# High and low weight products in pairs, first loads in halves, and dummy products at the start of a two-layer encoder

## The chip, the core and the metric

The kernel runs on one core of a Trainium2 chip. The metric is the device time of one execution in microseconds (us): 1684.95 us is the median of three runs of the kernel before (1684.54 to 1685.41). The core has a matrix engine (TensorE, in the profile PE for its products and PEld for its weight loads), VectorE (DVE), ScalarE (ACT), GpSimd (POOL) and a queue that issues transfers (SP). Products are summed in PSUM, everything else lies in SBUF, weights and inputs come from HBM by DMA.

## What is computed

Two layers of an encoder over 256 positions of 2048 channels, each a normalisation, one wide input projection, two groups of mixers and one output projection with a residual. Cut to the parts that set the work:

```python
def even_layer(h, w_in, w_out, ...):                      # w_in: 2048 x 14336
    a_q, a_i, a_ff, a_fb, a_g, b_u, b_g = split_cols(h @ w_in, EV_SIZES)
    a_out = hgrn2_mixer(a_q, a_i, a_ff, a_fb, lb, hgrn_nw) * jax.nn.silu(a_g)
    b_out = fourier_mixer(b_u, fw, fb) * jax.nn.silu(b_g)
    return jnp.concatenate([a_out, b_out], axis=-1) @ w_out   # 4096 x 2048

def odd_layer(h, w_in, w_out, ...):                       # w_in: 2048 x 13376
    c_in, c_b, c_c, c_g, d_z, d_xbc, d_dt = split_cols(h @ w_in, OD_SIZES)
    c_out = c_b * centred_dwconv(c_c * c_in, sconv_w) * jax.nn.silu(c_g)
    d_out = ssd_mixer(d_xbc, d_dt, d_z, ...)
    return jnp.concatenate([c_out, d_out], axis=-1) @ w_out

for layer in range(2):
    x = x + (even_layer if layer % 2 == 0 else odd_layer)(rms_norm(x, norm_w[layer]), ...)
return rms_norm(x, final_norm_w)
```

All of it is float32.

## The kernel before

**Two parts of each number.** The large products are made with a rounded 32-bit type. So that they stay exact enough, every weight and every activation is split in two: a high part (the rounded number) and a low part (what is left). A product then has three pieces: high weight by high activation, high weight by low activation, low weight by high activation. The activations of the first layer stand in the tile `xx`, 16 k tiles of 128 channels, each with its high half (256 positions) and its low half side by side. The mixers' outputs stand in `mm` in the same form.

**Weights come in halves.** `halves` lists all weight pieces in the order of their use: 562 pieces of 128 x 1024 numbers (512 KB), each being eight k tiles of 128 x 128. `load()` (L113) issues the transfer of a piece into one of five `raw` buffers from SP. `fetch()` (L121) makes the two parts of it: ACT copies `raw` into `hi` (L132), DVE subtracts to get `lo` (L133). There are three `hi`/`lo` buffer pairs (`NHL`), so ACT can write the high part of piece n + 3 only when the products have read that of piece n for the last time. `half()` (L152) hands out the next piece, runs whatever was put off with `later(n, ...)` to this piece, and fetches up to four pieces ahead.

**Three shapes of large product.** In `gemm_half` (L161) the weights are the stationary operand: for one piece, eight products of a high tile with 512 columns of `xx` (the high and the low activations together, L164), then eight products of a low tile with the 256 high activations (L167). All sixteen add into one PSUM bank. `gemm` calls it twice, `proj` gives a fresh bank. The even layer has 96 such projections (`pq`, two `pz`, `pu`, `pg`, `pbg`), the odd layer 105; so there are 402 calls of `gemm_half` and 3216 pairs of one high and one low product. The other two shapes have the activations stationary and always stream 512 columns of weights: the values `pv` (L508) and the output projections in `tproduct` (L183).

**Order.** Each engine runs its own list of instructions in order; a scheduler builds the lists from the program, so the written order is not always the order on an engine. Eight turns of `hp` make the even layer; each has, every other turn, `pv`, then for two heads `pq`, `pz`, `pz`, then `pu` twice, `pg` twice and `pbg` twice. Small products of the mixers (128 x 128, in plain float32) stand between the projections: `sa`/`sb`, `po`, `pt`, `fp`, `fm`, `fy`.

**The start.** SP issues `parT` (the small parameters, L258), then the first weight pieces and the eight chunks `x0` to `x7` of the input in turn (L263, L265). ACT and DVE split weights (L132, L133) and multiply the chunks by the norm weights into the two halves of `xx` (`split_by`, L223 and L224). ACT later squares the chunks in place for the norm (L276). The first products are those of `pv`: a unit of twelve for each piece, eight units.

Of the kernel before, what the change touches and what calls it, by code (L numbers as in the profile page):

```python
# [8 lines left out]
F32 = mybir.dt.float32  # L9
F32R = mybir.dt.float32r  # L10
U32 = mybir.dt.uint32
AF = mybir.ActivationFunctionType
ALU = mybir.AluOpType
ADD, SUB, MUL, MIN, MAX = ALU.add, ALU.subtract, ALU.mult, ALU.min, ALU.max

P = 128
# [40 lines left out]
def encoder_kernel(ctx: ExitStack, tc, xT, xN, w_ev, w_evo, w_od, w_odo, fw, fnr, par, con, acon, tric, outN):  # L57
    nc = tc.nc
    V, S, PE = nc.vector, nc.scalar, nc.tensor

    cpool = ctx.enter_context(tc.tile_pool(name="cpool", bufs=1))
# [9 lines left out]
    parT = cpool.tile([P, NPAR], F32, tag="par", name="parT")  # L71
# [7 lines left out]
    def pcol(name, i):  # L79
        return parT[:, PCOL[name] + i:PCOL[name] + i + 1]  # L80
# [9 lines left out]
    def t2(name, shape=(2, L)):  # L90
        return lpool[0].tile([P, *shape], F32, tag="t2", name=name, bufs=N2)

    def psum(tag, name, bufs, shape=(512,)):
        return ps.tile([P, *shape], F32, tag=tag, name=name, bufs=bufs)
# [4 lines left out]
    def paux(name, shape=(512,)):  # L99
        return psum("px", name, 8 - NPM, shape)  # L100
# [4 lines left out]
    n = 2 * (112 + 32)  # L105
# [2 lines left out]
    state = {"load": 0, "next": 0, "use": 0}  # L108
    HK = KT // 2
    NRAW, NHL, AHEAD = 5, 3, 4  # L110
    endp = []

    def load():  # L113
        n = state["load"]
        state["load"] = n + 1
        src, i, h = halves[n]
        raw = wpool.tile([P, HK * P], F32, tag=f"raw{n % NRAW}", name=f"raw{n}")
        nc.sync.dma_start(out=raw, in_=src[i][:, h * HK * P:(h + 1) * HK * P])
        loaded[n] = raw

    def fetch():  # L121
        n = state["next"]
        state["next"] = n + 1
        if n >= state["load"]:
            load()
        raw = loaded.pop(n)
        kept = n - (len(halves) - 8)
        i = n % NHL if kept < 0 else kept % (2 * NHL)
        pool = wpool if i < NHL else endp[0]
        hi = pool.tile([P, HK * P], F32R, tag=f"hi{i}", name=f"hi{n}")  # L130
        lo = pool.tile([P, HK * P], F32R, tag=f"lo{i}", name=f"lo{n}")
        S.activation(hi, raw, AF.Copy)  # L132
        V.tensor_tensor(lo, raw, hi.bitcast(F32), SUB)  # L133
        ready[n] = (hi, lo)

    def later(n, fn):
# [15 lines left out]
    def half():  # L152

        n = state["use"]
        due(n)
        while state["next"] <= min(n + AHEAD, len(halves) - 1):
            fetch()
        state["use"] = n + 1
        return ready.pop(n)

    def gemm_half(out, a, k0, first, last):  # L161
        hi, lo = half()
        for k in range(HK):
            PE.matmul(out, lhsT=hi[:, k * P:(k + 1) * P], rhs=a[:, k0 + k].rearrange("p s n -> p (s n)"),  # L164
                      start=(first and k == 0), stop=False)
        for k in range(HK):
            PE.matmul(out[:, :L], lhsT=lo[:, k * P:(k + 1) * P], rhs=a[:, k0 + k, 0], start=False,  # L167
                      stop=(last and k == HK - 1))

    def gemm(out, a):  # L170

        for h in range(2):
            gemm_half(out, a, h * HK, h == 0, h == 1)
# [43 lines left out]
    def split_by(dst, src, w=None):  # L217

        if w is None:
            S.activation(dst[:, 0], src, AF.Copy)  # L220
            V.tensor_tensor(dst[:, 1], src, dst[:, 0].bitcast(F32), SUB)
        else:
            S.activation(dst[:, 0], src, AF.Copy, scale=w)  # L223
            V.scalar_tensor_tensor(dst[:, 1], src, w, dst[:, 0].bitcast(F32), MUL, SUB)  # L224
# [30 lines left out]
    lay = ExitStack()  # L255
    ap_ = lay.enter_context(tc.tile_pool(name="ap", bufs=1))
    lpool.append(ap_)
    nc.sync.dma_start(out=parT, in_=par)  # L258
    V.memset(epsT, EPS)
    xcs = []  # L260
    for c in range(8):
        if c % 2 == 0:
            load()  # L263
        xc = t2(f"x{c}")
        nc.sync.dma_start(out=xc, in_=xT[:, 2 * c:2 * c + 2, :])  # L265
        xcs.append(xc)
    for c in range(8):
        if c % 2 == 0:
            fetch()
        for k in range(2):  # L270
            split_by(xx[:, 2 * c + k], xcs[c][:, k, :], pcol("nw0", 2 * c + k))
# [24 lines left out]
    with lay:  # L296
# [203 lines left out]
        for hp in range(8):  # L500
            if hp % 2 == 0:
                pv = [pmain(f"pv{hp}_{b}") for b in range(2)]
                for u in range(8):
                    hi, lo = half()
                    for k in range(2):
                        for b in range(2):
                            for n, (s_, w) in enumerate(((0, hi), (0, lo), (1, hi))):
                                PE.matmul(pv[b], lhsT=xx[:, 2 * u + k, s_, b * P:(b + 1) * P],  # L508
                                          rhs=w[:, k * 4 * P:(k + 1) * 4 * P], start=(u == 0 and k == 0 and n == 0),
                                          stop=(u == 7 and k == 1 and n == 2))  # L510
# [5 lines left out]
            for i in range(2):  # L516
                h = 2 * hp + i
# [15 lines left out]
            for i in range(2):  # L533
                h = 2 * hp + i
# [6 lines left out]


    ss1 = sp.tile([P, 2, 4], F32, tag="ss1", name="ss1")
    ones = cpool.tile([P, P], F32, tag="ones", name="ones")
    nc.gpsimd.memset(ones, 1.0)
    op = ctx.enter_context(tc.tile_pool(name="op", bufs=1))

    def tok(name, bufs=4):
# [27 lines left out]
    with ExitStack() as lay:  # L576
# [54 lines left out]
        for h in range(2):  # L631
            for out in (dtp, first_b):
                gemm_half(out, xx, h * HK, h == 0, h == 1)
# [300 lines left out]
```

## Time and profile before

| | us |
|---|---|
| median of three runs | 1684.95 |
| the profiled execution, whole | 1684.59 |
| its span on the core | 1682.8 |
| TensorE busy (PE) | 1666.2 (99%) |
| weight loads (PEld) | 1443.0 (86%) |
| VectorE busy | 1247.6 (74%) |
| ScalarE busy | 950.2 (56%) |
| bytes moved | 319.65 MB, mean 190 GB/s |

The span runs from the first to the last instruction of the program; 1.8 us of the profiled execution lie outside it. Busy times are unions of the instructions' stretches. Products are pipelined: one starts before the one ahead has ended, so the distance from start to start is what a product costs, and a busy share of 99% does not by itself say that each product is as short as it can be.

### The profile page before, as it was taken

The page shows a single profiled execution, that of the slowest core. Times are in us where ns is not written, and L with a number is a line of the kernel's source. Part 1 is how long each engine was busy: PE and PEld are TensorE (multiplying, and loading weights), DVE is VectorE, ACT ScalarE, POOL GpSimd, SP SyncE. Part 2 cuts the span into 40 slices and gives each one's busy share as a digit, 9 for nine tenths or more (in the row PEclk, how much of TensorE's full clock was granted, in tenths as well). Part 3 has the DMA queues.
Part 4 walks back from the last instruction along what each step waited for, and adds up shares of the span by engine and source line. Part 5 has one row for each costly group of instructions (what it writes and reads, how often), then busy time and mean ns, then how long its engine had stood idle before and what let it go on. Part 6 is the DMA issues. An engine that isn't in the chain of part 4 may idle for free.

```text
span 1682.8 us, 24794 instructions
## 1 busy us (share of the span) xinstructions
PE 1666.2 (99%) x9216; PEld 1443.0 (86%) x9216; DVE 1247.6 (74%) x2187; ACT 950.2 (56%) x1593; POOL 1.8 (0%) x13
## 2 busy tenths in 40 slices
PE   8999999999999999999999999999999999999997
PEld 6888888888888888888888888888888888888886
DVE  7868677867786788754548998888898797865554
ACT  6656555655665565644445576666665565654443
POOL 0000000000000000000000000000000000000000
PEclk9999999999999999999999999999999999999999
DMA  8555555545445545476665667656656655576553
GB/s 304 173 179 174 167 171 179 171 167 186 166 158 180 191 154 178 158 223 206 213 212 191 205 218 200 195 191 203 197 185 201 196 193 179 178 238 209 195 192 123
DMA packets 97977, 319.65 MB, mean 190 GB/s; under 512 B 10880, under 2 KB 19520, under 8 KB 97728
## 3 DMA queue, kind: packets, MB, share of 16 engines
q1 hardware_dynamic: 97856, 318.07, 57.5%
q8 instruction: 72, 1.18, 0.3%
q14 instruction: 49, 0.40, 0.1%
HBM read 313.77 MB, written 4.26 MB: 189 GB/s over the span
## 4 chain that ended last, share of the span: by engine, by line
PE 99%; DMA 0%; ACT 0%; DVE 0%; ACTq 0%; issue 0%; SPq 0%
PE pz L164 10%; PE o L183 10%; PE pz L167 5%; PE pv L508 5%; PE oD L183 5%; PE oC L183 5%; PE px L164 4%; PE pbg L164 4%; PE pq L164 4%; PE pcb L164 4%; PE pu L164 4%; PE pci L164 4%; PE pcg L164 3%; PE pcc L164 3%; PE pg L164 3%; PE pci L167 2%
## 5 line engine op out<-in xcount | busy, mean ns | idle before, releaser
L133 DVE TENSOR_TENSOR lo<-raw,hi 128x1024 fp32r<-128x1024 f32 x562 | 686.0, 1223 | 383.1 <-ACT hi L132 379.4
L132 ACT ACTIVATE hi<-raw 128x1024 fp32r<-128x1024 f32 x562 | 594.8, 1059 | 552.7 <-PE o L183 88.4
L164 PE MATMUL pz<-xx,hi 128*128 128x512 f32 x768 | 192.4, 393 | 0.0
L164 PEld LDWEIGHTS pz<-xx,hi 128*128 128x128 f32 x768 | 138.2, 189 | 24.5
L183 PE MATMUL o<-hi,mm 128*128 128x512 f32 x512 | 126.9, 390 | 0.0
L183 PEld LDWEIGHTS o<-hi,mm 128*128 128x128 f32 x512 | 95.8, 188 | 19.7
L167 PEld LDWEIGHTS pz<-xx,lo 128*128 128x128 f32 x768 | 104.8, 191 | 7.5
L167 PE MATMUL pz<-xx,lo 128*128 128x256 f32 x768 | 107.1, 283 | 0.0
L508 PE MATMUL pv<-hi,xx 128*128 128x512 f32 x256 | 81.9, 399 | 7.0 <-ACT xx L223 7.0
L183 PE MATMUL o<-lo,mm 128*128 128x512 f32 x256 | 68.5, 389 | 0.0
L164 PE MATMUL pbg<-xx,hi 128*128 128x512 f32 x256 | 66.2, 400 | 0.0
L164 PE MATMUL pcb<-xx,hi 128*128 128x512 f32 x256 | 65.5, 398 | 0.0
L164 PE MATMUL pg<-xx,hi 128*128 128x512 f32 x256 | 65.4, 398 | 0.0
L164 PE MATMUL px<-xx,hi 128*128 128x512 f32 x256 | 65.3, 397 | 0.0
L164 PE MATMUL pu<-xx,hi 128*128 128x512 f32 x256 | 64.8, 395 | 0.0
L164 PE MATMUL pci<-xx,hi 128*128 128x512 f32 x256 | 64.8, 395 | 0.0
L183 PE MATMUL oC<-hi,mm 128*128 128x512 f32 x256 | 64.5, 389 | 0.0
L164 PE MATMUL pq<-xx,hi 128*128 128x512 f32 x256 | 64.5, 394 | 0.0
L164 PE MATMUL pcc<-xx,hi 128*128 128x512 f32 x256 | 64.1, 393 | 0.0
L164 PE MATMUL pcg<-xx,hi 128*128 128x512 f32 x256 | 64.1, 393 | 0.0
L508 PEld LDWEIGHTS pv<-hi,xx 128*128 128x128 f32 x256 | 49.2, 192 | 17.3 <-ACT xx L223 7.0
L183 PE MATMUL oD<-hi,mm 128*128 128x512 f32 x256 | 63.4, 390 | 0.0
(551 smaller groups left out, 2851.0 us busy)
## 6 DMA issues: line engine op xcount, KB each, us to landing
raw<-in_w_ev SPq DMA_DIRECT2D x224, 512.0 KB, 3.9
raw<-in_w_od SPq DMA_DIRECT2D x210, 512.0 KB, 4.4
raw<-in_w_evo SPq DMA_DIRECT2D x64, 512.0 KB, 4.5
raw<-in_w_odo SPq DMA_DIRECT2D x64, 512.0 KB, 4.5
ab<-rd SPq DMA_DIRECT2D x64, 128.0 KB, 4.9
x<-in_xT SPq DMA_DIRECT2D x8, 256.0 KB, 6.9
fw<-in_fw SPq DMA_DIRECT2D x8, 256.0 KB, 5.9
xr<-in_xN SPq DMA_DIRECT2D x8, 256.0 KB, 5.8
```

The costliest lines, as they stand in the source:

```text
L132: S.activation(hi, raw, AF.Copy)
L133: V.tensor_tensor(lo, raw, hi.bitcast(F32), SUB)
L164: PE.matmul(out, lhsT=hi[:, k * P:(k + 1) * P], rhs=a[:, k0 + k].rearrange("p s n -> p (s n)"), start=(first and k == 0), stop=False)
L167: PE.matmul(out[:, :L], lhsT=lo[:, k * P:(k + 1) * P], rhs=a[:, k0 + k, 0], start=False, stop=(last and k == HK - 1))
L183: PE.matmul(outs[b], lhsT=a[:, k0 + 2 * u + k, s_, b * P:(b + 1) * P], rhs=w2[part][:, k * 4 * P:(k + 1) * 4 * P], start=(u == 0 and part ...
L508: PE.matmul(pv[b], lhsT=xx[:, 2 * u + k, s_, b * P:(b + 1) * P], rhs=w[:, k * 4 * P:(k + 1) * 4 * P], start=(u == 0 and k == 0 and n == 0) ...
```

## The change

- **Order of products.** In `gemm_half` the two loops become one: after each high product comes the low product of the same k tile.
- **First weight piece in halves.** `pieces(0)` gives two halves of 512 columns: two transfers, two ACT copies and two DVE subtractions for the first piece alone.
- **First input chunk in halves.** `x0` comes in two transfers of one k tile each.
- **Parameters in two parts.** The 16 columns of the first norm weight come first, the other 336 after `x1`.
- **Dummy products.** A tile of ones is set by DVE at the start (before, GpSimd set it; it is used later too), and 16 products of it with itself, 128 x 128 in float32, go into a PSUM bank that nobody reads.

```diff
+    def pieces(n):
+        return (slice(0, 512), slice(512, 1024)) if n == 0 else (slice(0, 1024),)
...
-        nc.sync.dma_start(out=raw, in_=src[i][:, h * HK * P:(h + 1) * HK * P])
+        for c in pieces(n):
+            nc.sync.dma_start(out=raw[:, c], in_=src[i][:, h * HK * P + c.start:h * HK * P + c.stop])
...
-        S.activation(hi, raw, AF.Copy)
-        V.tensor_tensor(lo, raw, hi.bitcast(F32), SUB)
+        for c in pieces(n):
+            S.activation(hi[:, c], raw[:, c], AF.Copy)
+            V.tensor_tensor(lo[:, c], raw[:, c], hi[:, c].bitcast(F32), SUB)
...
         for k in range(HK):
             PE.matmul(out, lhsT=hi[:, k * P:(k + 1) * P], rhs=a[:, k0 + k].rearrange("p s n -> p (s n)"),
                       start=(first and k == 0), stop=False)
-        for k in range(HK):
             PE.matmul(out[:, :L], lhsT=lo[:, k * P:(k + 1) * P], rhs=a[:, k0 + k, 0], start=False,
                       stop=(last and k == HK - 1))
...
-    nc.sync.dma_start(out=parT, in_=par)
+    ones = cpool.tile([P, P], F32, tag="ones", name="ones")
+    V.memset(ones, 1.0)
     V.memset(epsT, EPS)
+
+    warm = paux("warm")
+    for i in range(16):
+        PE.matmul(warm[:, :P], lhsT=ones, rhs=ones, start=True, stop=True)
+    nc.sync.dma_start(out=parT[:, :16], in_=par[:, :16])
     xcs = []
     for c in range(8):
         if c % 2 == 0:
             load()
         xc = t2(f"x{c}")
-        nc.sync.dma_start(out=xc, in_=xT[:, 2 * c:2 * c + 2, :])
+        for k in (slice(0, 1), slice(1, 2)) if c == 0 else (slice(0, 2),):
+            nc.sync.dma_start(out=xc[:, k], in_=xT[:, 2 * c + k.start:2 * c + k.stop, :])
         xcs.append(xc)
+        if c == 1:
+            nc.sync.dma_start(out=parT[:, 16:], in_=par[:, 16:])
...
-    ones = cpool.tile([P, P], F32, tag="ones", name="ones")
-    nc.gpsimd.memset(ones, 1.0)
```

**TensorE at the first projection** (`pq` of head 0, just after the values and the norm's small products; a name ends with a running number). Before:

```order
L242 MATMUL n_ms<-sq_x,conT 128x256
L288 MATMUL n_tok<-conT,sq_x 128x1 x2
L164 MATMUL pq_373<-xx,hi_259 128x512 x8
L167 MATMUL pq_373<-xx,lo_260 128x256 x8
L164 MATMUL pq_373<-xx,hi_294 128x512 x8
L167 MATMUL pq_373<-xx,lo_295 128x256 x8
```

With the change:

```order
L247 MATMUL n_ms<-sq_x,conT 128x256
L302 MATMUL n_tok<-conT,sq_x 128x1 x2
L170 MATMUL pq_397<-xx,hi_283 128x512
L172 MATMUL pq_397<-xx,lo_284 128x256
L170 MATMUL pq_397<-xx,hi_283 128x512
L172 MATMUL pq_397<-xx,lo_284 128x256
L170 MATMUL pq_397<-xx,hi_283 128x512
L172 MATMUL pq_397<-xx,lo_284 128x256
```

Each piece still has eight high and eight low products; the high tile is now read until the fifteenth of the sixteen, the low tile is wanted from the second.

**ScalarE at the start of the program**, from its table load to the second weight piece. Before:

```order
L68 ACT_TABLE_LOAD
L644 ACTIVATE aneg<-parT 64x1
L314 ACTIVATE lbe<-lbe 128x48
L132 ACTIVATE hi_110<-raw_86 128x1024
L223 ACTIVATE xx<-x_88,parT 128x256 x2
L223 ACTIVATE xx<-x_90,parT 128x256 x2
L276 ACTIVATE x_88<-x_88 128x512
L132 ACTIVATE hi_122<-raw_92 128x1024
```

With the change:

```order
L68 ACT_TABLE_LOAD
L138 ACTIVATE hi_132<-raw_105 128x512 x2
L228 ACTIVATE xx<-x_108,parT 128x256 x2
L228 ACTIVATE xx<-x_111,parT 128x256 x2
L290 ACTIVATE x_108<-x_108 128x512
L656 ACTIVATE aneg<-parT 64x1
L290 ACTIVATE x_111<-x_111 128x512
L328 ACTIVATE lbe<-lbe 128x48
L138 ACTIVATE hi_146<-raw_114 128x1024
```

The two small instructions on parameters and one more square have moved between the first and the second weight piece.

**SP at the start.** Before:

```order
L258 DMA parT<-in_par 128x352
L118 DMA raw_86<-in_w_ev 128x1024
L265 DMA x_88<-in_xT 128x512
L265 DMA x_90<-in_xT 128x512
L118 DMA raw_92<-in_w_ev 128x1024
```

With the change:

```order
L270 DMA parT<-in_par 128x16
L123 DMA raw_105<-in_w_ev 128x512 x2
L277 DMA x_108<-in_xT 128x256 x2
L277 DMA x_111<-in_xT 128x512
L280 DMA parT<-in_par 128x336
L123 DMA raw_114<-in_w_ev 128x1024
```

The large part of the parameters has moved behind the first two input chunks; the second weight piece has the same bytes ahead of it as before.

## Rows read from the trace of the kernel before

**Rows 1.** The page: TensorE's busy time, transfer rate by slice, engines of the chain.

```profile
PE 1666.2 (99%) x9216; PEld 1443.0 (86%) x9216; DVE 1247.6 (74%) x2187; ACT 950.2 (56%) x1593; POOL 1.8 (0%) x13
...
GB/s 304 173 179 174 167 171 179 171 167 186 166 158 180 191 154 178 158 223 206 213 212 191 205 218 200 195 191 203 197 185 201 196 193 179 178 238 209 195 192 123
...
PE 99%; DMA 0%; ACT 0%; DVE 0%; ACTq 0%; issue 0%; SPq 0%
```

**Rows 2.** Timeline of TensorE near 391 us: start us, length us, what.

```profile
391.02 2.00 PE L164 MATMUL pz<-xx,hi 128*128 128x512 f32 x8
392.86 1.12 PE L167 MATMUL pz<-xx,lo 128*128 128x256 f32 x8
393.81 2.00 PE L164 MATMUL pz<-xx,hi 128*128 128x512 f32 x8
```

**Rows 3.** Timeline of TensorE near 206 us, where a projection follows the values.

```profile
206.12 1.98 PE L164 MATMUL pq<-xx,hi 128*128 128x512 f32 x8
207.93 1.11 PE L167 MATMUL pq<-xx,lo 128*128 128x256 f32 x8
208.88 2.00 PE L164 MATMUL pq<-xx,hi 128*128 128x512 f32 x8
```

**Rows 4.** Groups of TensorE, 391.19 to 391.25 us: busy us, mean ns, idle before.

```profile
L164 PE MATMUL pz<-xx,hi 128*128 128x512 f32 x1 | 0.4, 397 | 0.0
```

**Rows 5.** Groups of TensorE, 392.90 to 392.97 us: last high, first low product.

```profile
L164 PE MATMUL pz<-xx,hi 128*128 128x512 f32 x1 | 0.4, 390 | 0.0
L167 PE MATMUL pz<-xx,lo 128*128 128x256 f32 x1 | 0.3, 278 | 0.0
```

**Rows 6.** Groups of TensorE, 393.40 to 393.45 us: two later low products.

```profile
L167 PE MATMUL pz<-xx,lo 128*128 128x256 f32 x2 | 0.4, 284 | 0.0
```

**Rows 7.** Timeline of all engines, first 22 us; in brackets idle time and its end.

```profile
5.50 1.06 ACT L132 ACTIVATE hi<-raw 128x1024 fp32r<-128x1024 f32 x1 [1.37 <-DMA raw<-in_w_ev]
...
6.58 1.23 DVE L133 TENSOR_TENSOR lo<-raw,hi 128x1024 fp32r<-128x1024 f32 x1 [1.34 <-ACT hi L132]
...
7.00 1.22 PE L508 MATMUL pv<-hi,xx 128*128 128x512 f32 x2 [7.00 <-ACT xx L223]
...
8.03 0.64 PE L508 MATMUL pv<-lo,xx 128*128 128x512 f32 x1
...
8.46 0.63 PE L508 MATMUL pv<-hi,xx 128*128 128x512 f32 x1
...
8.64 0.63 ACT L276 ACTIVATE x<-x 128x512 f32<-128x512 f32 x1 [0.49 <-DVE xx L224]
...
9.17 1.04 ACT L132 ACTIVATE hi<-raw 128x1024 fp32r<-128x1024 f32 x1
...
18.37 1.05 ACT L132 ACTIVATE hi<-raw 128x1024 fp32r<-128x1024 f32 x1
...
19.45 1.23 DVE L133 TENSOR_TENSOR lo<-raw,hi 128x1024 fp32r<-128x1024 f32 x1 [0.26 <-ACT hi L132]
...
21.02 0.39 PE L508 MATMUL pv<-lo,xx 128*128 128x512 f32 x1
```

**Rows 8.** Timeline of TensorE near 79 us, at the first `pg` projection.

```profile
78.81 1.06 PE L397 MATMUL po<-v,ST 128*128 128x128 f32 x8
79.63 2.09 PE L164 MATMUL pg<-xx,hi 128*128 128x512 f32 x8
81.56 1.11 PE L167 MATMUL pg<-xx,lo 128*128 128x256 f32 x8
```

**Rows 9.** Timeline of ScalarE near 70 us.

```profile
69.68 1.06 ACT L132 ACTIVATE hi<-raw 128x1024 fp32r<-128x1024 f32 x1 [0.18 <-PE pu L164]
```

**Rows 10.** Timeline of VectorE, 72 to 82 us.

```profile
72.81 0.69 DVE L338 TENSOR_TENSOR_SCAN B<-acT,G 128x256 f32<-128x256 f32 x1 [0.16 <-ACT G L336]
...
78.19 3.49 DVE L133 TENSOR_TENSOR lo<-raw,hi 128x1024 fp32r<-128x1024 f32 x3
```

**Rows 11.** Waits of the whole run: who for whom, us, times, longest us.

```profile
ACT hi L132 <- PE pu L164: 4.9, 16, 0.4
```

## The prediction

> **What bounds the kernel now.** I read the page first: TensorE is busy for 99% of the span, and the chain that ended last is TensorE's own work for 99% [rows 1]. So the end moves only by what TensorE's products cost from start to start, and by new waits in front of them. Its long wait is the first: it starts at 7.00 us, when ACT has written the first `xx` [rows 7]. Next I read the timeline where nothing but projections runs. A half (eight high and eight low products) takes 393.81 - 391.02 = 2.79 us, so a pair costs 349 ns. The high run takes 1.84 us, 230 ns a product; the low run 0.95 us, 119 ns a product [rows 2]. Then I looked for the same thing with another past. Behind the values, which stream 512 columns throughout, the high run takes only 1.81 us (226 ns each) and the half 2.76 us; the very next half, behind a low run, has its high run at 1.84 again [rows 3]. So 0.03 us of nearly every half is lost where a run of long products follows a run of short ones. The groups of single products show how: a product's recorded length runs past the start of the next by about as much for all of them, so differences of length are differences of cost. The first high product behind a low run has 397 ns, the last of the run 390 [rows 4, 5]; the first low product behind a high run has 278 ns, later ones 284 [rows 5, 6]. A high product thus costs 7 ns more right behind a low one than in a settled run, a low one 6 ns less right behind a high one.
>
> **The order of products.** Nothing is added or removed: 3216 pairs, each high product now right behind a low one and the reverse. No row shows single products of both lengths in turns, so I bound the pair from both sides.
> - If the loss at the turn vanishes because no short run builds up, a pair costs 2.76 / 8 = 345 ns: 3.75 ns less, 12.1 us over 3216 pairs.
> - If each product has the price it has now right behind the other kind, the high one costs 226 + 7 = 233 ns. The low one: with its first 6 ns shorter the low run is 0.95 us, so a settled one costs 0.956 / 8 = 119.5, and the first 113.5. The pair is 346.5 ns, 2.25 less than 348.75: 7.2 us.
> - If the high one keeps its +7 and the low one loses its -6, the pair is 352.5: 12.1 us more.
> I take the middle one, -7.2 us, because its two prices are those of exactly this neighbour; the ends stay for the range.
>
> **What the order does to buffers.** The high tile is now read to the fifteenth product. Before, the eighth high product starts 1.84 - 0.23 = 1.61 us into the half; now it starts after seven pairs, 7 x 0.3465 = 2.43 us. So each high buffer comes free 0.82 us later, and each low part is wanted one product after the first high one instead of eight. Mostly that is covered by what was fetched ahead. At one place it is not. At 69.68 us ACT has waited for just this release, by `pu` [rows 9]; behind its copy stand the exponentials of the head, whose result VectorE waits for at 72.81, and from there VectorE works without a gap to the three subtractions at 78.19 [rows 10]. The first of these, done at 78.19 + 1.23 = 79.42, is the low part for the `pg` half that TensorE starts at 79.63; before, it is wanted at 81.56 [rows 8]. Now ACT's copy, and with it this whole queue, ends 0.82 later, at 80.24. From the end of a subtraction to the low product that waited for it there are 8.03 - 7.81 = 0.22 us [rows 7], so the low product starts at 80.46. It could have started one high product after 79.63, which here, behind small products, is 1.93 - 1.61 = 0.32 us [rows 8, 2]: 79.95. The wait is 0.51 us. ACT's wait for `pu` comes 16 times, two for each of the eight `hp` turns [rows 11], so I count it eight times: +4.1 us. If some of the shift is absorbed it is 0; if none of the 0.82 is covered, 6.6.
>
> **The start.** The dummies: four `po` products of 128 x 128 in float32 are eight steps in 0.82 us [rows 8], so 16 dummies are 32 steps, 3.3 us at that pace and 6.6 at half of it. The first real products stand 8.46 - 8.03 = 0.43 us apart [rows 7], which for 512 columns is the lower of TensorE's two levels (1.2 GHz), later ones 0.23 (2.4 GHz). Dummies from about 1 us are over between 4.3 and 7.6 us, so they hardly hold up data that before came at 7.00, and the products behind them may run at the higher level at once. But that buys little, since supply is next: from 9.17 us ACT makes a weight piece, four `xx` and one square in (18.37 - 9.17) / 3 = 3.07 us without a gap, while a unit of twelve products at 0.227 takes 2.72. The fifth low part is done at 19.45 + 1.23 = 20.68 and used at 21.02 [rows 7]: 0.34 later, of which 0.22 is that same passage. So TensorE can gain 0.1 us there plus what ACT gains at its second weight piece (9.17 before). Ahead of the first chunk's end there are now 296 KB less, about 1.0 us at the first slice's 304 GB/s [rows 1]; but between its first and second weight piece ACT now does one more square (0.63) [rows 7] and the two small parameter instructions, which I put at less than a square together: 0.6 to 1.3 us. I take -0.2 us, between -1.1 (all of the earlier data kept) and +1.0 (none of it).
>
> **Sum.** -7.2 + 4.1 - 0.2 = -3.3 us. The profiled execution took 1684.6 us, 1682.8 of them span; I leave the 1.8 outside as they are: 1681.3. The median of the runs is 0.4 us above it, so I forecast 1681.6. A measurement of this kernel can tell about 0.2% (3.4 us) from no change, so this gain is at the edge of what shows.
>
> **The rivals.**
> - The loss at the turn goes away: -12.1 + 3.9 = -8.2, 1676.8 us. For it: the loss seems to need a run of short products, and there is none any more. Against it: the loss begins with the first high product, and that one's neighbour stays.
> - More is won: the high one settles at 226 ns and the low one keeps 113.5, a pair of 339.5, -29.7 + 3.9, 1659 us. For it: both prices are there in rows; against: never side by side.
> - The order does nothing: each product has one price, what start times show at the turns is given back by the neighbours, the pair stays at 349 ns and the waits and the start are left: +3.9, 1688.9 us, just on the slower side. For it: the +7 and the -6 nearly cancel. By the Trainium skill (TensorE: Matmul & The Clock Gate, section Back-to-back issue gap) the isolated distance of a product is its columns at the clock plus some 2.5 ns, which depends on nothing around it; that rule is this rival, though its level (216 and 109 ns, an estimate from the page, against 226 and 119 here) isn't the trace's.
> - Slower: the turn costs every time. The high product keeps +7 and the low one costs 119.5 in its weight load's shadow: 352.5 a pair, +12.1 + 3.9, 1701 us. It decides from a pair above 349 ns. For it: the extra cost of high products is spread over the run (230 against 226 in the mean), so it may be that one low product is enough to call it up.
>
> **How the numbers follow.** The forecast's case has 0.34 (half of it beyond 0.2%), the vanished loss 0.25, more won 0.09, order does nothing 0.14 (half of it beyond 0.2%), slower turns 0.18. That is faster 0.17 + 0.24 + 0.09 = 0.50, trimmed to 0.46 since the waits at `pg` may be longer; same 0.28; slower 0.26. The range leaves out the case of 1659 and the upper half of the slower turns: 1666 to 1697. The forecast's own range is 1677 to 1687.
>
> **What would show it.** Right: in the timeline of the changed kernel a half takes 2.77 us; the groups give high products near 397 and low ones near 278 ns; before the first low product of `pg` TensorE stands for about half a microsecond, eight times, released by VectorE's `lo`; the unit at 20 us starts within 0.5 us of before. Wrong: a half of 2.79 or above, no wait at `pg`, or waits at other projections, where I have taken the cover for granted.

## The result and the profile after

The changed kernel takes 1700.79 us (median of 4 runs, 1699.56 to 1701.23) against 1684.97 us for the kernel before on the same chip (4 runs, 1684.54 to 1685.41): a ratio of 1.0093 with a 95% interval of 1.0075 to 1.0110. It is slower by 15.8 us, where 3 us less was forecast. The profiled execution took 1701.2 us, 1699.4 of them span; the one of before 1684.6 and 1682.8. TensorE is as busy as before, with 18 us more of it on the page (compare [rows 1]), and its timeline has 6.7 us of them in dummies:

```profile
PE 1684.2 (99%) x9248; PEld 1442.5 (85%) x9248; DVE 1251.7 (74%) x2189; ACT 945.0 (56%) x1594; POOL 1.7 (0%) x12
...
PE 97%; DVE 1%; ACT 0%; DMA 0%; SPq 0%; issue 0%; ACTq 0%; DVEq 0%
```

```profile
1.05 6.72 PE L269 MATMUL warm<-ones 128*128 128x128 f32 x32 [1.05 <-DVE epsT L265]
```

The chain is still TensorE's; VectorE has 1% of it, where it had none. So the loss is to be looked for in what products cost from start to start, and in waits. The timeline of TensorE in the middle of the projections (start us, length us, what) shows the products of a half and the first one of the next:

```profile
393.00 0.40 PE L170 MATMUL pz<-xx,hi 128*128 128x512 f32 x1
393.24 0.28 PE L172 MATMUL pz<-xx,lo 128*128 128x256 f32 x1
393.35 0.40 PE L170 MATMUL pz<-xx,hi 128*128 128x512 f32 x1
...
393.70 0.40 PE L170 MATMUL pz<-xx,hi 128*128 128x512 f32 x1
...
394.06 0.40 PE L170 MATMUL pz<-xx,hi 128*128 128x512 f32 x1
...
395.82 0.40 PE L170 MATMUL pz<-xx,hi 128*128 128x512 f32 x1
```

Three pairs take 394.06 - 393.00 = 1.06 us, and eight 395.82 - 393.00 = 2.82, where the kernel before took 2.79 [rows 2]. The exact start times repeat every three pairs: a high product costs 241, 236, 233 ns in turn, the low one behind it 120, 113, 117. That is 353.3 ns a pair. In the same kernel, behind the small products at 258 us, the same code runs at another pace:

```profile
259.32 0.40 PE L170 MATMUL pg<-xx,hi 128*128 128x512 f32 x1
259.55 0.28 PE L172 MATMUL pg<-xx,lo 128*128 128x256 f32 x1
259.67 0.40 PE L170 MATMUL pg<-xx,hi 128*128 128x512 f32 x1
...
260.02 0.39 PE L170 MATMUL pg<-xx,hi 128*128 128x512 f32 x1
...
260.37 0.39 PE L170 MATMUL pg<-xx,hi 128*128 128x512 f32 x1
...
260.71 0.39 PE L170 MATMUL pg<-xx,hi 128*128 128x512 f32 x1
```

Four pairs take 260.71 - 259.32 = 1.39 us: high products of 230 to 233 ns and low ones of 112 to 117, repeating every pair or two, 346.7 ns a pair. I call 353.3 the slow cadence and 346.7 the fast one. By the start times of the last six pairs of each half, 281 of the 398 halves that no other product interrupts stand in the slow cadence, 117 in the fast one, and a half in an uninterrupted run of projections is always in the cadence of the half ahead of it (305 of 305). In the middle of a run of projections the eight-by-eight order has one pace: 349.2 ns a pair.

The account, by start times against the kernel before, is this. The first `pq` product starts 34.69 - 32.24 = 2.45 us later. All halves from their second product to the product that follows, with the small products between them, take 10.9 us more. Of these, 7.0 are the cadences (281 halves at 33 ns more, 117 at 20 less), 1.6 stand at the ends of the eight turns, and the other 2.3 are spread over places where the projections meet small products or the wait at `pg`. The distance from a half's first product to its second takes 2.75 us more in sum, and nearly all of that is the first `pg` half of the eight turns. The tail behind the last projection takes 0.5 us more. The sum is 16.6, the difference of the spans.

The `pg` place, in TensorE's timeline and in the list of waits (who for whom, us, times, longest us), against [rows 8, 11]:

```profile
82.59 0.47 PE L170 MATMUL pg<-xx,hi 128*128 128x512 f32 x1
83.16 0.39 PE L172 MATMUL pg<-xx,lo 128*128 128x256 f32 x1
```

```profile
ACT hi L138 <- PE pu L170: 5.6, 16, 0.5
...
PEld pg L172 <- DVE lo L139: 3.9, 8, 0.6
```

From the first high product to the first low one there are 0.57 us in four of the eight turns (83.16 - 82.59 here) and 0.73 in the other four, where about 0.31 would do: 0.26 and 0.42 us of waiting, 2.7 us in all. The released weight load names VectorE's `lo`, eight times, and ACT still waits for `pu` 16 times.

At the end of each of the eight turns there is a wait that the kernel before does not have. The two small `pt` products stand there for ScalarE's `on`, some 0.2 us each time, 1.6 us in all by the start times:

```profile
PEld pt L426 <- ACT on L420: 1.3, 8, 0.2
```

The start, in the timeline of ACT and of TensorE (in brackets the idle time and what ended it), against [rows 7]:

```profile
10.10 1.06 ACT L138 ACTIVATE hi<-raw 128x1024 fp32r<-128x1024 f32 x1
12.46 1.71 ACT L228 ACTIVATE xx<-x,parT 128x256 fp32r<-128x256 f32 x4 [1.30 <-DMA x<-in_xT]
```

```profile
34.69 0.48 PE L170 MATMUL pq<-xx,hi 128*128 128x512 f32 x1
```

The first `pq` product of the kernel before:

```profile
32.24 0.94 PE L164 MATMUL pq<-xx,hi 128*128 128x512 f32 x3
```

The first products now stand 0.23 us apart, not 0.43, but ACT's second weight piece comes at 10.10 (9.17 before), and then ACT stands 1.30 us for the third input chunk, a wait that the start of before does not have. The dummies also hold the first product up: the last of their 32 steps starts at 7.50 us and the first `pv` product at 7.53 (7.00 before), though the same loads without dummies let it start at 6.39.

### The profile page after: what moved, and what is told of

Its sections match the earlier page's. It is cut to its first block, busy times and chain, and to the rows that moved or that the text cites. A ratio compares the mean times of both kernels' runs of the same rounds, so it can differ in the third digit from the quotient of the medians.

```text
span 1699.4 us, 24851 instructions
## 1 busy us (share of the span) xinstructions
PE 1684.2 (99%) x9248; PEld 1442.5 (85%) x9248; DVE 1251.7 (74%) x2189; ACT 945.0 (56%) x1594; POOL 1.7 (0%) x12
## 4 chain that ended last, share of the span: by engine, by line
PE 97%; DVE 1%; ACT 0%; DMA 0%; SPq 0%; issue 0%; ACTq 0%; DVEq 0%
PE pz L170 11%; PE o L188 10%; PE pz L172 5%; PE oD L188 5%; PE oC L188 5%; PE pv L522 4%; PE px L170 4%; PE pq L170 4%; PE pci L170 4%; PE pcc L170 4%; PE pbg L170 3%; PE pcb L170 3%; PE pcg L170 3%; PE pu L170 3%; PE pg L170 3%; PE pg L172 2%
## 5 line engine op out<-in xcount | busy, mean ns | idle before, releaser
L139 DVE TENSOR_TENSOR lo<-raw,hi 128x1024 fp32r<-128x1024 f32 (+1 forms) x563 | 686.7, 1222 | 381.7 <-ACT hi L138 377.6
L138 ACT ACTIVATE hi<-raw 128x1024 fp32r<-128x1024 f32 (+1 forms) x563 | 595.0, 1057 | 588.9 <-PE pz L170 95.5
L170 PE MATMUL pz<-xx,hi 128*128 128x512 f32 x768 | 272.8, 399 | 0.0
L172 PE MATMUL pz<-xx,lo 128*128 128x256 f32 x768 | 215.9, 281 | 0.0
L172 PEld LDWEIGHTS pz<-xx,lo 128*128 128x128 f32 x768 | 145.3, 189 | 0.0
L170 PE MATMUL px<-xx,hi 128*128 128x512 f32 x256 | 92.5, 402 | 0.0
L172 PE MATMUL pg<-xx,lo 128*128 128x256 f32 x256 | 72.7, 284 | 1.4 <-DVE lo L139 1.0
L172 PE MATMUL pci<-xx,lo 128*128 128x256 f32 x256 | 72.5, 283 | 0.0
L172 PE MATMUL pq<-xx,lo 128*128 128x256 f32 x256 | 72.0, 281 | 0.0
L172 PE MATMUL px<-xx,lo 128*128 128x256 f32 x256 | 71.9, 281 | 0.0
```

What stands on the lines that cost most here:

```text
L138: S.activation(hi[:, c], raw[:, c], AF.Copy)
L139: V.tensor_tensor(lo[:, c], raw[:, c], hi[:, c].bitcast(F32), SUB)
```

## The experiments

Each kernel was timed beside the kernel before on the same chip. Its median was between 1684.6 and 1684.9 us there each time. "The order" is the one product after the other of the changed kernel; line numbers are each kernel's own.

**The order alone.** The kernel before with the two loops of `gemm_half` made one, and nothing else.

```diff
         for k in range(HK):
             PE.matmul(out, lhsT=hi[:, k * P:(k + 1) * P], rhs=a[:, k0 + k].rearrange("p s n -> p (s n)"),
                       start=(first and k == 0), stop=False)
-        for k in range(HK):
             PE.matmul(out[:, :L], lhsT=lo[:, k * P:(k + 1) * P], rhs=a[:, k0 + k, 0], start=False,
                       stop=(last and k == HK - 1))
```

> The kernel before with only the order of products changed (high and low in turns), the start as before. Theory A (cadence): the products in turns run at 353.3 ns a pair in most halves (2827 ns a half against 2793 before) and at 346.7 in the others, +7.1 us in sum, and waits at pg and elsewhere add 4 to 6; so +11 to +13 us, 1696 to 1698. Rival B (the order costs nothing by itself, the start does the harm): +3 to +4 us from the waits alone, 1688 to 1689, with halves of 2.79 us.

1698.90 us (1698.04 to 1699.37), ratio 1.0081 [1.0068, 1.0095], 14.0 us more. 286 halves stand in the slow cadence, 112 in the fast one. Theory A holds, with a time a little above its 1696 to 1698; B falls.

**The start alone.** The changed kernel with the two loops of before.

> The changed kernel with the old order of products (eight by eight); dummies, halves of the first loads and split parameters stay. Theory A: the start costs what the first pq shows, 34.69 against 32.24 us, so +2.4 us, 1687.4. Rival B: the start costs more later (buffers or queues out of step), +10 us or more. Rival C: the loss at the start needs the new order, 0 us.

1687.34 us (1686.82 to 1688.20), ratio 1.0014 [1.0005, 1.0023], 2.4 us more; halves of 2793 ns in the middle of the runs, as before. The two parts add up: 14.0 + 2.4 = 16.4, against 15.8 measured for the whole change.

**Two and two.** High, high, low, low: half as many changes of kind as in the order, four times as many as before. Here and in the next orders a list of turns takes the place of the two loops.

```diff
-        for k in range(HK):
...
-        for k in range(HK):
...
+        turns = [(k, low) for j in range(0, HK, 2) for low in (0, 1) for k in (j, j + 1)]
+        for n, (k, low) in enumerate(turns):
+            if low:
+                PE.matmul(out[:, :L], lhsT=lo[:, k * P:(k + 1) * P], rhs=a[:, k0 + k, 0], start=False,
+                          stop=(last and n == 2 * HK - 1))
+            else:
+                PE.matmul(out, lhsT=hi[:, k * P:(k + 1) * P], rhs=a[:, k0 + k].rearrange("p s n -> p (s n)"),
+                          start=(first and k == 0), stop=(last and n == 2 * HK - 1))
```

> The kernel before with products in the order high, high, low, low: four turns in a half instead of one (before) or eight (changed). Theory A1 (each turn from low to high costs what it costs before, some 21 ns): a half of 2793 + 63 ns, +25 us with no waits. Theory A2 (short groups settle in a cadence of their own, each turn costs 0 or 6.7 ns): a half between 2773 and 2800 ns, -8 to +3 us, plus 2 to 4 us of waits. Rival B (order neutral): 0 to +4 us from the waits.

1685.35 us, ratio 1.0002 [0.9993, 1.0012]. TensorE's timeline:

```profile
392.97 0.63 PE L169 MATMUL pz<-xx,hi 128*128 128x512 f32 x2
393.44 0.40 PE L166 MATMUL pz<-xx,lo 128*128 128x256 f32 x2
393.67 0.63 PE L169 MATMUL pz<-xx,hi 128*128 128x512 f32 x2
...
395.76 0.62 PE L169 MATMUL pz<-xx,hi 128*128 128x512 f32 x2
```

Sixteen products take 395.76 - 392.97 = 2.79 us, by the exact starts 2786.7 ns: 6.7 less than before, with eight changes of kind in the half instead of two. Theory A1 falls: a change of kind has no price of its own. The time shows nothing of the shorter halves, whose 6.7 ns would be 2.7 us if all 402 had them. What costs is the rhythm as a whole: 241/120/236/113/233/117 is dear, 232/231/113/120/233/236/116/112 is not.

**Runs of one kind twice as long.** The second half of each projection runs its eight lows first, then its eight highs, so that highs follow highs and lows follow lows.

```diff
+        turns = [(k, low) for low in ((1, 0) if last else (0, 1)) for k in range(HK)]
```

> The kernel before with the second half of each projection in the order low, then high: low runs meet low runs and high runs meet high runs, so half as many turns (201 instead of 402 from low to high). Theory A (a turn after a long low run costs 21 ns): -4.2 us, 1680.8, with high runs of 1.81 us in first halves that follow a high run. Rival B (order neutral): 0 us. Rival C (the low parts of second halves are wanted 1.8 us sooner and their high buffers come free 1 us later): waits of up to 0.5 us in some projections, 0 to +8 us.

1689.97 us, ratio 1.0030 [1.0018, 1.0041]. The halves do what theory A says: those whose highs follow highs take 2766 ns, the others 2801, ten less in the mean. The loss is elsewhere, in TensorE's timeline at 79 us:

```profile
79.03 0.39 PE L169 MATMUL pg<-xx,hi 128*128 128x512 f32 x1
79.90 0.49 PE L399 MATMUL po<-v,ST 128*128 128x128 f32 x2 [0.49 <-DVE ST L392]
80.15 0.70 PE L169 MATMUL pg<-xx,hi 128*128 128x512 f32 x2
80.69 0.90 PE L399 MATMUL po<-v,ST 128*128 128x128 f32 x6
```

The scheduler now puts the small `po` products inside the first `pg` half; they wait for VectorE, whose chain runs some 3 us later (the first scan at 76.02, 72.81 before [rows 10]). That is 0.8 us in each of eight turns.

**The same way in for each half.** The order, but each half begins with two highs and two lows.

```diff
+        turns = [(0, 0), (1, 0), (0, 1), (1, 1)] + [(k, low) for k in range(2, HK) for low in (0, 1)]
```

> The kernel before, with only the order of a half's products changed: each half begins with two highs and two lows, and the other six pairs stand in turns as in the changed kernel. Theory A (products in turns fall into one of two cadences, 346.7 or 353.3 ns a pair, and what stands ahead of the turns sets which): every half now has the same way in, so the halves in the middle of the projections all take the same time, without a mix: 697 + 6 x 346.7 = 2777 ns if it is the fast cadence (1682 us in all with some waits at pg), 697 + 6 x 353.3 = 2817 if it is the slow one (1695 us). Theory B (the cadence is set by something else that persists, such as which buffers or banks are in use): about 7 of 10 halves stay at 2817, the others at 2777, 1692 us.

1690.58 us, ratio 1.0035 [1.0021, 1.0049]. Neither: 187 halves are slow and 211 fast, and in the long uninterrupted runs (of twelve and of seven halves) they alternate slow, fast, slow, fast, 188 times out of 189. Of all 305 pairs of adjoining halves 276 change; most of the others stand in runs of two and of five. Two halves that follow each other:

```profile
393.31 0.63 PE L169 MATMUL pz<-xx,hi 128*128 128x512 f32 x2
393.78 0.40 PE L166 MATMUL pz<-xx,lo 128*128 128x256 f32 x2
...
396.13 0.40 PE L169 MATMUL pz<-xx,hi 128*128 128x512 f32 x1
```

```profile
396.13 0.63 PE L169 MATMUL pz<-xx,hi 128*128 128x512 f32 x2
396.60 0.39 PE L166 MATMUL pz<-xx,lo 128*128 128x256 f32 x2
...
398.91 0.40 PE L169 MATMUL pq<-xx,hi 128*128 128x512 f32 x1
```

The first takes 396.13 - 393.31 = 2.82 us, the second 398.91 - 396.13 = 2.78. My theory was too simple: the way in does not set the cadence, it turns the one that is there into the other. The cadence is a state that products in turns hand on, and in the long runs two highs with two lows flip it.

**A fourth pair of buffers.** The order, with four `hi`/`lo` pairs and, for room, three raw buffers.

```diff
-    NRAW, NHL, AHEAD = 5, 3, 4
+    NRAW, NHL, AHEAD = 3, 4, 4
```

> The changed kernel's order of products in the kernel before's start, with four pairs of high and low buffers in the place of three, and three buffers for raw weights in the place of five to make room. If the waits at the first pg half (0.26 and 0.42 us, eight in all, 2.7 us) come from the high buffers' later release, they go, and the halves keep their two cadences: 1698.9 - 2.7, 1696 us. If they come from something else (the low part wanted seven products earlier, whatever the buffers), they stay: 1699 us. If the raw buffers are now too few, new waits for DMA appear ahead of the copies, above 1699.

1693.47 us, ratio 1.0055 [1.0041, 1.0069], 5.4 us less than the order alone. At `pg` the wait is gone in TensorE's timeline, and no line of the waits has TensorE waiting at `pg` any more:

```profile
81.00 0.47 PE L164 MATMUL pg<-xx,hi 128*128 128x512 f32 x1
81.31 0.28 PE L166 MATMUL pg<-xx,lo 128*128 128x256 f32 x1
```

From high to low there are 0.31 us. So the wait hung on the high and low buffers, as the prediction had it. The fourth pair does not bring VectorE's queue forward (its three subtractions begin at 80.79 us, 80.75 in the order alone); it lets the low part of this half be made one piece sooner, at 73.37, ahead of that queue. In the order alone the eight waits at `pg` are 2.2 us (0.26 in seven turns, 0.42 in one). Of the 1.6 us at the ends of the turns 1.1 go too. Besides, 49 fewer halves stand in the slow cadence (237 slow, 164 fast), 49 x 54 ns = 2.6 us, which nobody planned. Together these are 5.9 us; small losses elsewhere take 0.5 back.

**The long runs with four buffers.** The order of the run with long runs of one kind, with four `hi`/`lo` pairs and three raw buffers.

```diff
-    NRAW, NHL, AHEAD = 5, 3, 4
+    NRAW, NHL, AHEAD = 3, 4, 4
...
+        turns = [(k, low) for low in ((1, 0) if last else (0, 1)) for k in range(HK)]
```

> The kernel before, with the second half of each projection running its eight lows first and then its eight highs, as in the earlier run of this order, but with four pairs of high and low buffers and three raw ones. Half of the halves then stand behind a run of highs and take 2766 ns, the others 2801, 10 ns a half less than before, 4 us in all. If the earlier run lost its gain at the place of pg (0.8 us, eight times) to the later release of the high buffers, that loss goes and the time is 1681 us; if the loss stays, 1690.

1697.58 us, ratio 1.0078 [1.0063, 1.0094]. The halves keep their 10 ns. In the list of waits:

```profile
PE po L399 <- DVE ST L392: 5.1, 8, 1.7
PE cb L763 <- DVE C1s_e L253: 2.7, 1, 2.7
```

At `pg` the loss grows in the first turn alone, where `po` waits 1.7 us: ACT's copy at 70.80 waits for its transfer there, with three raw buffers in the place of five. In the other seven turns `po` waits 0.48 us as in the run with three pairs, and ACT's copy ahead of it still waits 2.28 us for `pu`. So a fourth pair does not take that loss away; what would was not tried. Most of the time above that run lies elsewhere: 3.0 us in the odd layer where `cb` waits for VectorE, and 1.3 us behind the last projection.

**The start with the parameters whole.** The start of the changed kernel and the order of before, with the parameters in one transfer and first.

```diff
-    nc.sync.dma_start(out=parT[:, :16], in_=par[:, :16])
+    nc.sync.dma_start(out=parT, in_=par)
...
-        if c == 1:
-            nc.sync.dma_start(out=parT[:, 16:], in_=par[:, 16:])
```

> The changed kernel's start (dummy products, first weight piece and first chunk in halves) with the kernel before's order of products, but with the parameters loaded whole and first, as in the kernel before. If the 2.4 us of the changed start come from the parameters' late second part (two small instructions and a square then stand between ACT's first and second weight piece), the first pq half starts within 0.5 us of the kernel before, 32.2 to 32.7 us, and the time is 1685. If they come from the halved loads or the dummies, the time stays at 1687.3.

1687.03 us (11 runs, 1685.64 to 1688.73), ratio 1.0015 [1.0006, 1.0024]: the loss stays, so the parameters' second part is not its cause.

**One exchange in a run.** With four buffers and the order, the second half of 29 uninterrupted runs begins with two highs and two lows; all else stands in turns.

```diff
         turns = [(k, low) for k in range(HK) for low in (0, 1)]
+        if g in TWOS:
+            turns[1], turns[2] = turns[2], turns[1]
```

> The run with products in turns and four high and low buffer pairs, with one exchange more: in 29 uninterrupted runs of projections that stood in the slow cadence there (the 8 of twelve halves and 7 of four in the even layer, 14 of seven and four in the odd one), the second half begins with two highs and two lows instead of a high, a low, a high, a low; everything else stands in turns. Theory A' (a run keeps the cadence it is in until something breaks the turns, and two highs, two lows within a run always change it to the other one, as between the halves of the run before): in each of the 29 the first half stays at about 2827 ns and the other 3, 6 or 11 go to 2773, some 190 halves by 54 ns, 10 us less than that run: 1683 us, below the kernel before. Theory B' (the cadence belongs to the place, and the exchange at every half only shifted it by its own pair): the halves after the exchanged one fall back to 2827, 1692 to 1693 us. If the runs that follow a changed one start in another cadence than they did, the gain is smaller but the 29 still show their change.

1685.45 us, ratio 1.0005 [0.9996, 1.0014], 8.0 us less than the same kernel without the exchanges. 97 halves are slow and 304 fast, 140 fewer slow ones, 140 x 54 ns = 7.6 us. (`TWOS` holds the 29 of the 402 halves.) TensorE's timeline at one of the places:

```profile
1012.15 0.40 PE L175 MATMUL px<-xx,hi 128*128 128x512 f32 x1
...
1013.21 0.40 PE L175 MATMUL px<-xx,hi 128*128 128x512 f32 x1
...
1014.27 0.63 PE L175 MATMUL pz<-xx,hi 128*128 128x512 f32 x2
1014.73 0.39 PE L172 MATMUL pz<-xx,lo 128*128 128x256 f32 x2
1014.96 0.40 PE L175 MATMUL pz<-xx,hi 128*128 128x512 f32 x1
...
1016.70 0.39 PE L175 MATMUL pz<-xx,hi 128*128 128x512 f32 x1
```

Ahead of the exchange three pairs take 1013.21 - 1012.15 = 1.06 us, behind it five take 1016.70 - 1014.96 = 1.74: 353 and 348 ns a pair. In 28 of the 29 runs the cadence changed at the exchange and stayed changed to the end of the run. Seven of these went the wrong way: the runs of four halves behind a run of twelve came in fast now, because the run ahead was fast, and were turned to slow. The one that did not change met the exchange at another point of the slow cycle (ahead of its 236 ns product; the others ahead of the 233 or the 241). Theory A' holds, with "always" cut down to that; its 1683 us counted on some 190 halves.

**The dummies alone.** The kernel before with `ones` and the 16 dummy products.

> The kernel before with the 16 dummy products of ones ahead of the first data, and with nothing else of the change: loads, parameters and order of products are as before. If the changed start's 2.4 us come from the dummies, this one shows them: 1687, first pq half at 34 us. If they come from the halved loads: the first products run at 0.23 us from the start instead of 0.43, a gain of under a microsecond that supply gives back, 1684.5 to 1685.

1685.10 us, ratio 1.0001 [0.9993, 1.0010]. No loss and no gain, though the first product starts at 7.38 us, 0.38 later.

**The halved loads without the dummies.**

> The changed kernel's start without the dummy products (first weight piece, first chunk and parameters loaded in two parts), with the kernel before's order of products. If the 2.4 us come from the loads in parts, they are all here: 1687.3, the second x chunk lands around 12 us or later, first pq half at 34 us. If they come from the dummies: 1685.

1686.92 us, ratio 1.0013 [1.0004, 1.0022], 2.2 us more. The loss is in the halved loads: the first weight piece and the first chunk, since the run with the parameters whole has it too. ACT's timeline shows the wait for the third chunk again:

```profile
9.88 1.06 ACT L138 ACTIVATE hi<-raw 128x1024 fp32r<-128x1024 f32 x1 [0.26 <-DMA raw<-in_w_ev]
12.15 1.31 ACT L229 ACTIVATE xx<-x,parT 128x256 fp32r<-128x256 f32 x3 [1.21 <-DMA x<-in_xT]
```

**Exchanges placed by what was seen.** Four buffers and the order, with the seven wrong exchanges taken out and three added in the odd layer.

```diff
-    TWOS = ([24 * i + 1 for i in range(8)] + [24 * i + 13 for i in range(8) if i != 1] +
-            [215, 236, 248, 264, 276, 288, 300, 316, 328, 340, 352, 368, 380, 392])
+    TWOS = ([24 * i + 1 for i in range(8)] +
+            [203, 215, 236, 248, 255, 264, 276, 288, 300, 307, 316, 328, 340, 352, 368, 380, 392])
```

> The run before with its exchanges put by what that run showed: the seven ahead of the runs of four halves in the even layer are taken out (those stood in the fast cadence already and were turned to the slow one), and three are added in runs of the odd layer that stood in the slow one (the second halves from 912, 1067 and 1218 us). By theory A' the seven runs of four halves stay in the fast cadence (21 halves), and the runs of twelve and of four halves at the added places change in their second half, with the four to seven halves behind the first of them following as they did when it was fast: 45 to 50 halves by 54 ns, 2.5 us less than that run, 1683 us, 0.1% under the kernel before. If the runs' ways in differ from what those two runs showed, some of it is missing: 1684 to 1685.

1685.98 us (11 runs, 1684.45 to 1688.17), ratio 1.0008 [0.9999, 1.0017]: nothing gained. Six of the seven runs came in fast and stayed so, and one of the three new exchanges turned its run the right way. The other two runs came in fast this time and were turned to slow: 86 halves are slow, 315 fast, 11 better, 0.6 us by the cadences. The profiled execution lost more than that in waits of TensorE: `oC` waits 1.0 us for ACT, 0.2 in the run before, and `sa`, `fp`, `cb`, `pv` and `fy` wait 0.4 to 0.7 us each where that run has no such wait. Which cadence a run comes in with depends on what stood ahead of it, down to single waits; exchanges at fixed places do not hold it.

## Why the prediction was wrong

**The price of a pair.** This is the step that failed. I took a pair in turns as 233 + 113.5 = 346.5 ns and 7.2 us less, "because its two prices are those of exactly this neighbour". The groups of single products came out close to what I had named (397 and 278), 399 ns for a high and 281 for a low one in the mean:

```profile
L170 PE MATMUL pz<-xx,hi 128*128 128x512 f32 x768 | 272.8, 399 | 0.0
L172 PE MATMUL pz<-xx,lo 128*128 128x256 f32 x768 | 215.9, 281 | 0.0
```

That is no hit: 2 and 3 ns too much make 5 ns a pair, twice the 2.25 that I had hoped to win. A product's price does not depend on the one ahead of it alone. In the kernel before, the highs behind a low run cost 233, 236, 228, 232 and 231 ns by the exact starts (means of 232 halves) and only then 226 or 227; the lows behind a high run cost 113.5 and then 119 to 120. TensorE takes several products to settle, so prices of single products after a long run of the other kind cannot be put together into a new rhythm. In turns it falls into one of two cycles. The fast one is my 346.5 almost to the digit (346.7), the slow one is near the 352.5 of the rival "the turn costs every time" (353.3); both agree in the sum and not in the single prices, and that is luck in part. Some 70% of the halves took the slow one, and with the others' gain taken off, 7.0 us more came of it, where 7.2 less was forecast. The choice between the two bounds was made by a reason that the rows could not bear. The rival had 0.18 and 1701 us, close to the 1700.8 measured; the range had left out its upper half.

**The rivals.** "The loss at the turn goes away" falls: high products cost 230 to 241 ns in turns, never 226 in either cycle. "More is won" falls with it. "The order does nothing" falls by the first run: the order alone costs 14.0 us. The rule named there (the Trainium skill, TensorE: Matmul & The Clock Gate, section Back-to-back issue gap), by which an isolated product's distance hangs on its columns and the clock alone, does not describe these runs: the same product of 256 columns costs 112 to 120 ns here, by the rhythm that it stands in.

**The wait at `pg`.** Right in place, mechanism and count. ACT's copy that waits for `pu` starts 82.59 - 73.38 = 9.21 us ahead of that half, where it was 9.95 [rows 8, 9]: 0.74 us later, 0.82 forecast. The wait was 0.26 and 0.42 us instead of 0.51, 2.7 us in the sum instead of 4.1. A fourth pair of buffers took it away. What I had taken for covered was not so everywhere: the waits of `pt` at the ends of the turns cost another 1.6 us, and my sign for a wrong forecast, "waits at other projections", stood for just that.

**The start.** Outside the bounds I had set (-1.1 to +1.0): +2.45 us in the traces, +2.4 in the runs of the start alone. That the dummies would buy little is right: alone they change nothing. That they would hardly hold up the data is not: they start the first product at 7.53 us instead of 6.39, and give that back because the products behind them stand 0.23 us apart from the second on. A reading was off as well: the 296 KB less hold ahead of the first half of the first chunk; ahead of the whole chunk there are 168 KB less. What I missed is the price of more and smaller transfers. SP takes some 0.46 us for each issue. The second weight piece is the eighth of them, at 4.01 us, where before it was the fifth, at 2.59:

```profile
4.01 0.43 SPq L123 DMA_DIRECT2D raw<-in_w_ev  x1
```

```profile
2.59 0.43 SPq L118 DMA_DIRECT2D raw<-in_w_ev  x1
```

The rows of stretches (from and to in us, length, then busy time and instructions of PE, PEld, DVE, ACT and POOL, granted clock, DMA share, GB/s) show what followed, first in the kernel after, then in the one before:

```profile
2.00:4.00 2.00, 2.00 (x12) 2.00 (x11) 0.00 (x0) 0.02 (x1) 0.00 (x0) 1.00 0.72 160
6.00:8.00 2.00, 2.00 (x13) 1.96 (x13) 2.00 (x5) 1.97 (x6) 0.00 (x0) 1.00 0.91 249
```

```profile
2.00:4.00 2.00, 0.00 (x0) 0.00 (x0) 0.75 (x7) 0.34 (x3) 0.04 (x2) 1.00 0.93 233
6.00:8.00 2.00, 1.00 (x2) 0.64 (x3) 1.42 (x2) 2.00 (x5) 0.00 (x0) 1.00 0.96 344
```

From 2 to 4 us the transfer engines had less to do (0.72 of the time against 0.93) and moved 160 GB/s instead of 233; from 6 to 8 us they were nearly as busy as before (0.91 against 0.96) and moved 249 instead of 344. The Trainium skill (DMA: Bandwidth & Descriptors, section 🎯 Rules for kernel authors) tells to join many small transfers into a large one, and names 64 KB as the size under which overhead prevails. The run of the halved loads goes the same way, by 2.2 us, with parts of 256 and 128 KB. I had counted bytes ahead of the first chunk, and not what the extra issues do to the pieces behind. How the 2.2 us divide between late issue, small packets and the halves of the weight piece and of the chunk was not tried. The kernels whose loads are unchanged have their first `pq` between 32.2 and 33.6 us, and the one of before is the earliest of them, so a single trace tells the start to about a microsecond only; the 2 us rest on ten runs and more.

**The sum.** -3.3 us was forecast: -7.2, +4.1, -0.2. Measured are +10.9 (7.0 of them the cadences, the term that I had at -7.2), +2.75, +2.45 and 0.5 in the tail, 16.6 in the traces. The range, up to 1697, held all but the upper half of one rival and no start above +1.0; both happened together.

## What to carry to other kernels

The cost of a product from start to start belongs to the rhythm that it stands in: time a new order of products by a run of that order, not by adding up prices of neighbours taken from another one. Where rows give one bound on each side of the present pace and no row lies between them, nothing in the rows prefers the one, and the forecast should weigh them nearly alike. Where loads are cut up to start earlier, count the issues ahead of every later piece: here the third chunk came so late that more was lost than the first half piece had gained.

## What was not expected of the hardware

- Products of 512 and 256 columns in turns run in one of two steady cycles, 353.3 ns a pair (three pairs long) and 346.7, with the granted clock shown at full speed in both. In the changed kernel the cycle is handed on from half to half over new weights and other PSUM banks, 305 times out of 305. Two highs and two lows in between turn it into the other in 28 of 29 places, and 188 times out of 189 in the long runs of the kernel with the same way in. What in TensorE holds this state, and why small products or a wait let it come out as they do, stays open.
- Behind dummy products the real ones stood 0.23 us apart from the second on. Without them, with the same loads, the first products from 6.39 us on took 0.43 each until about 10.8 us, the lower of the two levels by their distance, while the granted clock of both stretches reads 1.00.
- More changes of kind can cost less: two and two, with eight changes a half, take 2786.7 ns; eight and eight, with two, 2793.
